# A two-block transformer on one core: retention's projections ahead of MLA attention, MLA on buffers of its own, retention in chunks with states

## The chip, the cores and the metric

The kernel runs on one core of one Trainium2 chip. The metric is the device time of one execution in microseconds (us); the median of three runs stands for a kernel. Engines are named as in the profile: PE (TensorE, matrix products), DVE (VectorE), ACT (ScalarE), POOL (GpSimd) and SP (SyncE, whose queue issues nearly all DMAs).

## The reference, cut to what matters

512 tokens of 1024 features pass a first block (two layers of windowed and full attention, untouched here) and a second block of two layers. Each of these projects the normed input and feeds three mixers (RWKV, retention, MLA attention), whose outputs, side by side, pass one output projection:

```python
for l in range(DEPTH):
    hn = rms_norm_2(h, attn_norm[l])
    proj = hn @ w_in[l]
    ...
    y_a, v_first = rwkv7_mixer(p_a, ...)
    y_b = retention_mixer(p_b, positions)
    y_c = mla_mixer(p_c, positions, ...)
    mix = jnp.concatenate([y_a.astype(h.dtype), y_b.astype(h.dtype), y_c.astype(h.dtype)], axis=-1)
    h = h + mix @ w_out[l]
    hn = rms_norm_2(h, ffn_norm[l])
    gu = hn @ w_gate_up[l]
    h = h + (jax.nn.silu(gu[..., :D_FF_2]) * gu[..., D_FF_2:]) @ w_down[l]
```

Retention (4 heads of 64) is defined in chunks of 128 tokens with a state handed from chunk to chunk; with one decay per head this equals one masked product over all 512 tokens:

```python
inner = jnp.einsum('bhnqd,bhnkd->bhnqk', qc, kc) * dmask[:, None]
inner = jnp.einsum('bhnqk,bhnkd->bhnqd', inner, vc)
kv_chunk = jnp.einsum('bhnkd,bhnke->nbhde', kc * k_dec[:, None, :, None], vc)
def step(R, kv_i):
    return R * chunk_dec[None, :, None, None] + kv_i, R
_, R_prev = lax.scan(step, R0, kv_chunk)
cross = jnp.einsum('bhnqd,nbhde->bhnqe', qc * q_dec[:, None, :, None], R_prev)
y = (inner + cross).transpose(0, 2, 3, 1, 4).reshape(B, S, RET_HEADS, RET_HEAD_DIM)
y = y * lax.rsqrt(jnp.mean(y * y, axis=-1, keepdims=True) + NORM_EPS)
return jax.nn.silu(g) * y.reshape(B, S, RET_DIM)
```

MLA attention has 8 heads (64 + 32 features for scores, 64 for values), causal over the 512 tokens.

## The kernel before

Activations lie with features on the partitions, in eight tiles of 128 x 512. A large product is made of split factors: `load_w` loads a weight (`raw`, two buffers), ACT casts it to `whi`, DVE subtracts to `wlo` (three buffers each); PE multiplies high with high, low with high and high with low. So a 1024 x 128 piece of a projection is 24 matmuls of 512 columns. `H` (tiles `hh`, `hl`) is the normed input of a layer in split form, `mix` (`mh`, `ml`) the mixers' output.

The program text gives the work and the buffers; when the program is built, a scheduler puts the instructions of each engine into one fixed order, in which the engine then runs them. Pools of SBUF tiles and of PSUM banks (`psum`, `bank(tag)`, 8 banks in all) decide when a buffer may be written again.

In `block2`, one layer's mixers run like this:

- `rwkv`, with four PSUM banks `r`, and on its side `mla_inputs`, whose products alternate over the banks `l` and `b` (two each; `self.lb`). MLA's q, k and v go to DRAM (`mlaq`, `mlak`, `mlakr`, `mlav`), RWKV's output to `mix` in DRAM.
- `ret_inputs`, retention's own projections of `H`: four for q and k with a rotary step (`rope`: a shuffle, two products on DVE, one on POOL), one token-wise for v (96 matmuls of 256 columns) and two for the gate g. It is a generator: some of it is called ahead of MLA, the rest after it in the text, and the scheduler uses it as filling within MLA.
- `mla`, head by head: q, k and v come back from DRAM into the tiles of x (`slots`; x itself waits in DRAM as `xd`), ACT casts and DVE subtracts (`qk`). Scores go to the banks `l`, `l`, `m` in turn, DVE takes the row maximum, ACT the exponent, PE turns the result (bank `t`), ACT and DVE split it (`mpt`), PE multiplies with v (bank `o`). After each pair of heads the row sums go to DRAM and back as a broadcast (`rm`, `bc`), POOL multiplies, and SP stores the pair to `mix`.
- `retention`, two pairs of heads: for each pair a table of decays (`dec`, 512 KB) is loaded; per block of 128 keys, scores against all later queries (banks `l`, `l`, `m`), a multiplication by the table on DVE (`rp`), a product with v into `o`.
- `residual`: x comes back, `mix` is loaded and split, and eight pieces of the output projection are added to x, in the banks `b`: 18 matmuls each for the six tiles of RWKV and MLA, and behind them six each for retention's two tiles (`w2outb`), 192 in all.

Of the kernel before, what the change touches and what calls it, by code (L numbers as in the profile page):

```python
# [10 lines left out]
F32 = mybir.dt.float32  # L11
# [9 lines left out]
T = 512  # L21
# [33 lines left out]
class Kern:  # L55
    def __init__(self, tc, d, out, ctx, V):
        self.tc, self.nc, self.d, self.out = tc, tc.nc, d, out
        self.ctx, self.V = ctx, V
        nc = self.nc
        self.uid = 0  # L60
        E = ctx.enter_context
        self.const = E(tc.tile_pool(name="const", bufs=1))
        self.wp = E(tc.tile_pool(name="wp", bufs=2))
        self.tmp = E(tc.tile_pool(name="tmp", bufs=2))
        self.dram = E(tc.tile_pool(name="dram", bufs=1, space=DRAM))
        c = self.const
# [764 lines left out]
    def residual(self, wd, nkt, a, x, gcol, plan, done, norm=None, pre=None):  # L831
# [4 lines left out]
        for ns, segs in plan:  # L836
# [8 lines left out]
            for i, s in enumerate(segs):  # L845
                late = sum(n < KD - W_BUFS for n in ns) if i and len(ns) > 1 else 0
                for j, n in enumerate(ns[late:] + ns[:late]):
                    ps = self.bank()[:, :s.n]
# [732 lines left out]
    def retention(self, l, pool, src, mix):  # L1581
        nc = self.nc
        qk, vs, gs = src
        tags = itertools.cycle("llm")
        for p in range(2):
            q, k, g = qk[p], qk[2 + p], gs[p]
            dec = self.t(pool, [128, 2, T], F32, "dec", 1)
            nc.sync.dma_start(out=dec, in_=self.d["dec"][:, 2 * p:2 * p + 2])
            pso = self.bank("o")
            for j in range(4):  # L1590
                n = T - 128 * j
                ts = []
                for h in range(2):
                    hs = slice(64 * h, 64 * h + 64)
                    ps = self.bank(next(tags))[:, :n]
                    self.mm(ps, k[hs, 128 * j:128 * j + 128], q[hs, 128 * j:], True, True)
                    t = self.t(pool, [128, T], F32, "rp", 3)[:, :n]
                    nc.vector.tensor_tensor(t, ps, dec[:, h, :n], op=ALU.mult)
                    ts.append(t)
                for h in range(2):  # L1600
                    self.mm(pso[64 * h:64 * h + 64, 128 * j:], vs[j][:, 128 * p + 64 * h:128 * p + 64 * h + 64], ts[h], j == 0, j == 3)
# [8 lines left out]
    def mla(self, l, pool, slots, src, mix):  # L1610
        nc = self.nc
        rd = self.dram.tile([4, 2, 4, 128], F32, name=f"rm{l}")
        tags = itertools.cycle("llm")
        ring = {k: itertools.cycle([slots[i] for i in v]) for k, v in dict(f=(2, 3), P=(1, 5, 6, 4), y=(0,)).items()}
        self.fin = iter(())
        steps = [[] for _ in range(sum(MLAG) + 1)]
        for h in range(8):
            if h % 2 == 0:
# [5 lines left out]
                yt = next(ring["y"])  # L1624
                sums = self.t(pool, [128, 8], F32, "sums", 2)
            qk = []
            for nm in "qk":
                f = next(ring["f"])[0:96]
# [11 lines left out]
            for pair in range(2):  # L1640
                for ii in range(2):
                    i = 2 * pair + ii
                    n = 128 * (i + 1)
                    Sp = self.bank(next(tags))
# [5 lines left out]
                    P = next(ring["P"])  # L1650
# [3 lines left out]
                    def turned(P=P, i=i, ii=ii, pair=pair, out=out):  # L1654
                        if ii == 0:
                            out[pair] = [self.t(pool, [128, 4, 256], F32R, "mpt", 4) for _ in range(2)]
# [31 lines left out]
    def block2(self):  # L1688
# [28 lines left out]
        for l in range(2):  # L1717
# [3 lines left out]
            with ExitStack() as es:  # L1721
                es_l = ExitStack()
# [21 lines left out]
                es_r, es_mix, es_ps = (ExitStack() for _ in range(3))  # L1744
                rps = [self.pool(es_r, "ret0", "right")]
                self.lo = "vector"
                inputs = self.ret_inputs(l, rps, H, bc, rs, tab_r)
# [3 lines left out]
                rps.append(self.pool(es_r, "ret", "right"))  # L1751
# [16 lines left out]
            es_r.close()  # L1768
# [13 lines left out]
            self.residual(lambda n, k0, kn: d[f"w2out{l}"][n], 6, mix, X, 1, self.plan([LAT]), None)  # L1782
# [13 lines left out]
            es_mix.close()  # L1796
            es_b = ExitStack()
# [68 lines left out]
def constants():  # L1866
# [29 lines left out]
    df = np.arange(T)[None, :] - np.arange(128)[:, None]  # L1896
    dec = np.where(df[:, None, :] >= 0, np.exp(lg[None, :, None] * np.maximum(df, 0)[:, None, :]), 0.0) / 8.0
# [125 lines left out]
```

## Time and profile before

| what | us |
|---|---|
| median of three runs (3426.10 to 3429.61) | 3428.77 |
| the profiled execution | 3428.67 |
| its span in the trace | 3426.9 |
| PE busy in the span | 3322.7 (97%) |
| DVE, ACT, POOL busy | 1940.2, 1225.8, 498.3 |

The mixers of the second block's first layer run from about 1949 to 2301 us, those of its second from about 2686 to 3038 us:

| stage | first layer, us | second layer, us |
|---|---|---|
| RWKV, MLA's inputs | 184.0 | 184.3 |
| first 24 matmuls of `ret_inputs` | 7.2 | 7.5 |
| MLA attention | 67.3 | 67.3 |
| rest of `ret_inputs` | 24.4 | 24.3 |
| retention, output projection | 69.5 | 69.0 |

Read it so: PE is nearly always busy, so a stage's length is PE's work plus its waits; the other engines count where PE waits for them. In rows of a timeline, the columns are the start, the duration of the group, the engine, the line of the program, the operation, output<-input, tile shape and count, and in brackets the idle time ahead with what ended it.

### The profile page before, as it was taken

The numbers are of one execution on the slowest core, as the hardware profiler recorded it, in microseconds if no ns is written. First come the engines' busy times: TensorE is split into PE (matmuls) and PEld (weight loads), VectorE is DVE, ScalarE is ACT, GpSimd is POOL, SyncE is SP. The second block draws the span as 40 slices with busy tenths as digits, with TensorE's granted clock in tenths as the row PEclk, the third lists the DMA queues.
The fourth block names the chain that finished last, engine by engine and source line by source line (L and its number), as shares of the span: only waits on it lengthen the run. The fifth ranks groups of instructions, "written<-read, shape, count | busy, mean of one in ns | idle before, by whom it ended". The sixth has DMA issues, their size and how long they took to land. (4 is left out here: it accounts for less than half of the span.)

```text
span 3426.9 us, 48765 instructions
## 1 busy us (share of the span) xinstructions
PE 3322.7 (97%) x19304; PEld 2740.8 (80%) x19304; DVE 1940.2 (57%) x3306; ACT 1225.8 (36%) x2178; POOL 498.3 (15%) x430
## 2 busy tenths in 40 slices
PE   7999999999999999999999998999999988999998
PEld 4888888888888888888888876768888766678887
DVE  7667775756444567666333466764434666654333
ACT  3566622312222356634222322632223324433222
POOL 4231100100000201101000332211001332121001
PEclk9999999999999999999999999999999999999999
DMA  6433372434344243353333422422333214333332
GB/s 213 131 121 117 118 264 95 122 111 138 115 136 130 82 125 95 117 176 99 96 90 97 124 66 74 140 94 92 92 96 105 88 53 128 113 88 99 91 98 83
DMA packets 138397, 386.63 MB, mean 113 GB/s; under 512 B 17524, under 2 KB 29300, under 8 KB 138168
## 3 DMA queue, kind: packets, MB, share of 16 engines
q1 hardware_dynamic: 134840, 372.94, 35.5%
q0 software_dynamic: 3328, 10.57, 0.9%
q8 instruction: 152, 2.49, 0.3%
q14 instruction: 77, 0.63, 0.1%
HBM read 332.34 MB, written 43.76 MB: 110 GB/s over the span
## 5 line engine op out<-in xcount | busy, mean ns | idle before, releaser
L137 ACT CAST whi<-raw 128x1024 fp32r<-128x1024 f32 (+3 forms) x436 | 435.7, 999 | 1280.9 <-PE b L146 838.9
L146 PE MATMUL b<-hl,whi 128*128 128x512 f32 (+1 forms) x1760 | 687.1, 390 | 6.1 <-DVE hl L1089 5.1
L138 DVE TENSOR_TENSOR wlo<-raw,whi 128x1024 fp32r<-128x1024 f32 (+2 forms) x397 | 480.7, 1211 | 370.1 <-ACT whi L137 343.7
L146 PE MATMUL b<-hh,whi 128*128 128x512 f32 (+1 forms) x1760 | 687.4, 391 | 2.1 <-ACT whi L137 2.1
L146 PE MATMUL b<-hh,wlo 128*128 128x512 f32 (+1 forms) x1760 | 685.2, 389 | 1.1 <-DVE wlo L138 1.1
L146 PEld LDWEIGHTS b<-hl,whi 128*128 128x128 f32 x1760 | 332.1, 189 | 81.2 <-DVE hl L1089 8.1
L146 PEld LDWEIGHTS b<-hh,whi 128*128 128x128 f32 x1760 | 332.3, 189 | 77.7 <-ACT whi L137 3.1
L146 PEld LDWEIGHTS b<-hh,wlo 128*128 128x128 f32 x1760 | 332.2, 189 | 75.9 <-DVE wlo L138 1.9
L146 PE MATMUL b<-ah,whi 128*128 128x512 f32 (+1 forms) x864 | 317.8, 368 | 0.0
L146 PE MATMUL b<-ah,wlo 128*128 128x512 f32 (+1 forms) x864 | 317.7, 368 | 0.0
L146 PE MATMUL b<-al,whi 128*128 128x512 f32 (+1 forms) x864 | 317.6, 368 | 0.0
L146 PEld LDWEIGHTS b<-ah,whi 128*128 128x128 f32 x864 | 162.3, 188 | 30.0
L146 PEld LDWEIGHTS b<-ah,wlo 128*128 128x128 f32 x864 | 162.3, 188 | 29.8
L146 PEld LDWEIGHTS b<-al,whi 128*128 128x128 f32 x864 | 162.2, 188 | 29.9
L396 DVE SCALAR_TENSOR_TENSOR wlo<-raw,silb 128x1024 f32<-128x1024 f32 x128 | 158.0, 1235 | 47.0 <-DMA raw<-in_ada1b 27.4
L930 DVE TENSOR_TENSOR tm<-tm,b 128x512 f32<-128x512 f32 (+1 forms) x112 | 69.9, 624 | 198.7 <-PE b L146 192.6
L146 PE MATMUL l<-hh,whi 128*128 128x512 f32 (+1 forms) x472 | 176.6, 374 | 0.8 <-DVE stB L685 0.3
L146 PE MATMUL l<-hl,whi 128*128 128x512 f32 (+1 forms) x472 | 174.9, 371 | 0.0
L146 PE MATMUL l<-hh,wlo 128*128 128x512 f32 (+1 forms) x472 | 172.8, 366 | 0.0
L496 DVE TENSOR_TENSOR pt<-t,pt 128x384 fp32r<-128x384 f32 (+2 forms) x272 | 131.1, 511 | 36.7 <-ACT pt L495 34.9
L146 PE MATMUL b<-hc,whi 128*128 128x256 f32 x800 | 141.6, 280 | 0.0
L455 DVE TENSOR_REDUCE st<-S 128x1 f32<-128x768 f32 (+2 forms) x160 | 121.7, 763 | 34.0 <-PE S L146 33.4
(555 smaller groups left out, 5932.9 us busy)
## 6 DMA issues: line engine op xcount, KB each, us to landing
raw<-in_wgu SPq DMA_DIRECT2D x92, 512.0 KB, 3.6
raw<-in_w2gu SPq DMA_DIRECT2D x88, 512.0 KB, 3.5
raw<-in_ada1b SPq DMA_DIRECT2D x48, 512.0 KB, 3.6
raw<-in_w2in SPq DMA_DIRECT2D x38, 512.0 KB, 3.6
raw<-in_ada0b SPq DMA_DIRECT2D x32, 512.0 KB, 3.7
raw<-in_wg SPq DMA_DIRECT2D x32, 512.0 KB, 3.7
raw<-in_w2d SPq DMA_DIRECT2D x32, 512.0 KB, 3.5
raw<-in_wd SPq DMA_DIRECT2D x24, 512.0 KB, 3.6
```

The source lines that it names most:

```text
L137: self.nc.scalar.copy(hi, raw)
L138: getattr(self.nc, self.lo).tensor_tensor(lo, raw, hi.bitcast(F32), op=ALU.subtract)
L146: self.nc.tensor.matmul(out, l, r, start=start, stop=stop)
L396: nc.vector.scalar_tensor_tensor(junk, raw, 0.5, self.silb[:, v], op0=ALU.mult, op1=ALU.mult, accum_out=m[:, w, k, v:v + 1])
L455: nc.vector.tensor_reduce(nm, S[:, lo:hi], axis=AX.X, op=ALU.max, negate=True)
L496: nc.vector.tensor_tensor(o, src, h.bitcast(F32), op=ALU.subtract)
L930: nc.vector.tensor_tensor(b, th, pu, op=ALU.mult)
```

## The change

1. `ret_inputs` runs in full ahead of `mla`; `H` is then given up and made anew after it.
2. `mla` gets buffers of its own: `mf`, `mP`, `my` and two kinds of `mpt` in a pool of its own, in place of the tiles of x. So x can come back from DRAM earlier, and the output projection (`residual`) can begin while MLA runs.
3. PSUM: from the start of the layer on, `b` two banks, `t` two, `o` one, and RWKV three `r` (before: four); `mla_inputs` alternates over `b` and `t`; MLA's scores use `b` alone; when RWKV's buffers close, three banks `w` take the output projection.
4. `retention` works in chunks: scores only within a chunk, states of 64 x 64 from scaled keys (`rkt`), two steps from state to state (`rst`), and a product of states with scaled queries (`rq`). One table of 128 x 1280 (640 KB) is loaded for both pairs.

```diff
-        self.lb = itertools.cycle("lb")
+        self.lb = itertools.cycle("bt")
...
+        tab = self.t(pool, [128, 10, 128], F32, "dec", 1)
+        nc.sync.dma_start(out=tab, in_=self.d["dec"])
...
-            dec = self.t(pool, [128, 2, T], F32, "dec", 1)
-            nc.sync.dma_start(out=dec, in_=self.d["dec"][:, 2 * p:2 * p + 2])
+            nc.gpsimd.tensor_tensor(qd, v4(q)[:, 1:], tab[:, 6 + p].unsqueeze(1).to_broadcast([128, 3, 128]), op=ALU.mult)
+            ps = self.bank("t")
+            for c in range(3):
+                self.turn(v4(ps)[:, c], v4(k)[:, c])
+            kt = self.t(pool, [128, 3, 128], F32, "rkt", 2)
+            nc.vector.tensor_tensor(kt, v4(ps)[:, 0:3], tab[:, 4 + p].unsqueeze(1).to_broadcast([128, 3, 128]), op=ALU.mult)
+            inner = [self.bank("b") for _ in range(2)]
+            for c in range(4):
+                for h in range(2):
+                    self.mm(v4(inner[h])[:, c], v4(k)[hs[h], c], v4(q)[hs[h], c], True, True)
+            st = self.bank("t")[:, :192].rearrange("p (c e) -> p c e", e=64)
+            for c in range(3):
+                for h in range(2):
+                    self.mm(st[hs[h], c], kt[:, c, hs[h]], val(c, h), True, True)
...
+            nc.scalar.copy(R[:, 0], st[:, 0])
+            for c in (1, 2):
+                nc.vector.scalar_tensor_tensor(R[:, c], R[:, c - 1], tab[:, 8 + p, 0:1], st[:, c], op0=ALU.mult, op1=ALU.add)
             pso = self.bank("o")
...
+                    self.mm(v4(pso)[hs[h], c], val(c, h), v4(w[h])[:, c], c == 0, False)
+            for c in range(3):
                 for h in range(2):
-                    self.mm(pso[64 * h:64 * h + 64, 128 * j:], vs[j][:, 128 * p + 64 * h:128 * p + 64 * h + 64], ts[h], j == 0, j == 3)
+                    self.mm(v4(pso)[hs[h], c + 1], R[hs[h], c], qd[hs[h], c], False, c == 2)
...
-                    Sp = self.bank(next(tags))
+                    Sp = self.bank("b")
...
-                self.psum(es, r=4)
-                self.psum(es_l, "right", l=2, b=2)
-                rp = self.pool(es, "rw")
+            self.psum(es_l, "right", b=2, t=2, o=1)
+            self.psum(es_rw, r=3)
...
-                next(inputs)
-            self.psum(es_ps, t=2, o=1, m=1)
+                ri = self.run(self.ret_inputs(l, [retp, retp], H, bc, rs, tab_r))
+            es_H.close()
             with ExitStack() as es:
                 self.stream = "A"
-                self.mla(l, self.pool(es, "mla"), slots, sm, mixd)
+                self.mla(l, self.pool(es, "mla", "right"), sm, mixd)
                 self.stream = "L"
-            self.lo = "vector"
-            ri = self.run(inputs)
+            es_rw.close()
+            self.psum(es_ps, w=3)
```

Three places in the engines' orders, first layer. The first is ACT at the start of MLA. Before, the first casts of v, q and k (`mv`, `qk`) stand behind a weight that is free long before, and among PE's projections:

```order
L137 CAST whi_19912<-raw_19910 128x1024
L1622 CAST mv_19959<-vf_19957 128x8x64
L1635 CAST qk_3683_19964<-x_5145 96x512
L1635 CAST qk_3685_19970<-x_5146 96x512
L137 CAST whi_20701<-raw_20699 128x1024
```

After, on the same engine (`whi` of 128x768 are weights of the output projection, `tm<-rg` is the gate's tanh):

```order
L137 CAST whi_21344<-raw_21342 128x768
L1496 ACTIVATE tm_20214<-rg_20213 128x512
L137 CAST whi_21370<-raw_21368 128x768
L1496 ACTIVATE tm_20250<-rg_20249 128x512
L1642 CAST mv_20261<-vf_20259 128x8x64
L1655 CAST qk_3730_20268<-mf_20266 96x512
L1655 CAST qk_3733_20275<-mf_20272 96x512
```

The cast of `whi_21370`, whose buffer the last projection of `H` reads, and a tanh of that projection's result now stand ahead of the casts that the first scores need.

The second place is SP's queue at the end of MLA's last pair of heads: `rm` and `bc` carry the row sums, `mix` is the pair's store. Before:

```order
L469 DMA rm_19956<-rc_20689 8x128
L473 DMA bc_20692<-rm_19956 64x512 x2
L131 DMA raw_20971<-in_w2in 128x1024
L477 DMA mix_17969<-x_5143 128x512
L131 DMA raw_21237<-in_w2out 128x768
```

After:

```order
L469 DMA rm_20258<-rc_21043 8x128
L473 DMA bc_21046<-rm_20258 64x512 x2
L477 DMA mix_17969<-my_20825 128x512
L1588 DMA dec_21098<-in_dec 128x1280
L1798 DMA tm_21312<-mix_17969 128x512
```

Retention's only table load stands directly behind the last store; before, its two loads stand 40 rows ahead of this and 14 rows behind it.

The third place is PE at the start of retention. Before, with all projections of `H` done:

```order
L146 MATMUL l_21032<-rqk_19909,rqk_20698 128x512
L146 MATMUL l_21036<-rqk_19909,rqk_20698 128x512
L146 MATMUL m_21042<-rqk_19909,rqk_20698 128x384
L146 MATMUL b_21200<-cf,rst_18024 128x128 x3
L146 MATMUL o_21031<-rp_21034,rv_20852 64x512
L146 MATMUL o_21031<-rp_21038,rv_20852 64x512
```

After, from the last value product of MLA on (`w` is the output projection, `rkt` the keys scaled by the table):

```order
L146 MATMUL o_21018<-mpt_3962_21011,mv_20822 128x128
L146 MATMUL w_21322<-mh_21083,whi_21318 128x512
L146 MATMUL w_21348<-mh_21083,whi_21344 128x512
L146 MATMUL w_21374<-mh_21083,whi_21370 128x512
L146 MATMUL w_21322<-ml_21091,whi_21318 128x512
L146 MATMUL w_21322<-mh_21083,wlo_21319 128x512
L146 MATMUL w_21348<-ml_21091,whi_21344 128x512
L146 MATMUL w_21348<-mh_21083,wlo_21345 128x512
L146 MATMUL w_21374<-ml_21091,whi_21370 128x512
L146 MATMUL w_21374<-mh_21083,wlo_21371 128x512
L146 MATMUL t_21118<-rv_20099,rkt_21106 64x64 x2
```

Between MLA's last product and the first that needs the table stand nine matmuls of the output projection; the first score products and transposes of retention stand ahead of these value products. 147 further matmuls of the output projection follow. Of the 240 matmuls of `ret_inputs` that stood 24 ahead of, 64 within and 152 behind MLA, all are ahead of it now; 36 of the output projection stand within it.

## Rows read from the trace of the kernel before

**Rows 1.** The page's first part: busy time, share of the span, instructions.

```profile
PE 3322.7 (97%) x19304; PEld 2740.8 (80%) x19304; DVE 1940.2 (57%) x3306; ACT 1225.8 (36%) x2178; POOL 498.3 (15%) x430
```

**Rows 2.** Table by stretches, first layer: stretch, length, engines' busy times, PE clock, DMA.

```profile
1949.00:2133.00 184.00, 169.90 (x1701) 131.31 (x1699) 111.78 (x265) 46.53 (x79) 59.77 (x54) 0.94 0.23 66
2133.00:2140.20 7.20, 6.04 (x25) 4.53 (x25) 3.80 (x4) 2.32 (x4) 1.30 (x1) 1.00 0.75 204
2140.20:2207.50 67.30, 60.33 (x374) 47.78 (x373) 56.23 (x106) 48.34 (x129) 16.29 (x12) 0.97 0.48 147
2207.50:2231.90 24.40, 24.40 (x153) 21.59 (x151) 8.60 (x11) 6.84 (x11) 4.82 (x3) 1.00 0.36 115
2231.90:2301.40 69.50, 69.06 (x313) 46.52 (x313) 45.47 (x87) 22.69 (x33) 8.43 (x6) 1.00 0.30 95
2209.50:2219.50 10.00, 10.00 (x87) 10.00 (x86) 3.54 (x5) 2.42 (x5) 4.82 (x3) 1.00 0.35 122
```

**Rows 3.** Timeline of PE: first and last of 21 projection matmuls of 512 columns.

```profile
2135.30 0.40 PE L146 MATMUL b<-hh,whi 128*128 128x512 f32 x1
...
2139.97 0.39 PE L146 MATMUL b<-hh,wlo 128*128 128x512 f32 x1
```

**Rows 4.** Groups of DVE in the MLA stage: count, busy us, mean ns, idle before.

```profile
L1636 DVE TENSOR_TENSOR qk<-x,qk 96x512 fp32r<-96x512 f32 x14 | 13.2, 948 | 0.1
...
L138 DVE TENSOR_TENSOR wlo<-raw,whi 128x1024 fp32r<-128x1024 f32 x5 | 6.0, 1202 | 0.0
...
L437 DVE STREAM_SHUFFLE tm<-b 128x512 f32<-128x512 f32 x3 | 2.2, 736 | 0.0
```

**Rows 5.** One line's instructions (L1636, MLA stage): ns min/median/max, first and last start.

```profile
L1636 DVE TENSOR_TENSOR qk<-x,qk x14: 630/676/1801, 2143.9 to 2191.2; 96x512 fp32r<-96x512 f32 x14
```

**Rows 6.** Timelines of ACT and DVE at the start of MLA.

```profile
2135.75 0.62 ACT L1622 CAST mv<-vf 128x512 fp32r<-128x512 f32 x1 [2.10 <-DMA vf<-mlav]
2136.27 1.14 ACT L1635 CAST qk<-x 96x512 fp32r<-96x512 f32 x2
...
2136.92 1.97 DVE L1636 TENSOR_TENSOR qk<-x,qk 96x512 fp32r<-96x512 f32 x2 [1.41 <-ACT qk L1635]
```

**Rows 7.** Timelines of PE and SP at MLA's end; last, landing of the tables' DMAs.

```profile
2205.92 1.61 PE L146 MATMUL o<-mpt,mv 128*128 128x256 f32 x12 [1.22 <-DVE x L503]
...
2203.28 0.35 SPq L469 DMA_DIRECT2D rm<-rc  x1
...
2211.33 0.33 SPq L477 DMA_DIRECT2D mix<-x  x1
...
2241.62 0.33 SPq L1588 DMA_DIRECT2D dec<-in_dec  x1
...
DMA to landing us min/median/max: 3.6/3.6/3.6
```

**Rows 8.** Timeline of PE in retention: scores, successor, value products of 512 and 128 columns.

```profile
2231.93 1.13 PE L146 MATMUL l<-rqk,rqk 64*128 64x512 f32 x4
2232.89 0.81 PE L146 MATMUL m<-rqk,rqk 64*128 64x384 f32 x2
...
2234.93 1.67 PE L146 MATMUL o<-rp,rv 128*64 128x512 f32 x4 [0.36 <-DVE rp L1598]
...
2243.47 0.44 PE L146 MATMUL o<-rp,rv 128*64 128x128 f32 x4
```

**Rows 9.** Groups of PE by shape, from 2231.9 to 2301.4: retention's normalisation.

```profile
L146 PE MATMUL t<-cf,smlA 128*64 128x128 f32 x32 | 2.2, 279 | 0.0
L146 PE MATMUL t<-cf,ry 128*128 128x2 f32 x16 | 2.1, 254 | 0.1
```

**Rows 10.** Timeline of DVE in RWKV: two products consumed in a group.

```profile
2007.32 1.29 DVE L1317 TENSOR_TENSOR A<-r,m 128x512 f32<-128x512 f32 x2 [0.34 <-PE r L146]
```

**Rows 11.** PE's timeline around a gap, and the table by stretches behind it.

```profile
2122.31 1.98 PE L146 MATMUL r<-cf,smlR 128*64 128x128 f32 x16 [3.53 <-DVE smlR L217]
...
2121.30:2132.00 10.70, 9.69 (x33) 6.64 (x34) 4.71 (x11) 0.00 (x0) 0.00 (x0) 0.52 0.44 125
```

More of the change, by code (lines that the diff above doesn't have):

```diff
@@ L829, in merge, with residual @@
                 self.ada_some(1)
-    def residual(self, wd, nkt, a, x, gcol, plan, done, norm=None, pre=None):
+    def residual(self, wd, nkt, a, x, gcol, plan, done, norm=None, pre=None, tag="b"):
         nc = self.nc
@@ L847, in residual @@
                 for j, n in enumerate(ns[late:] + ns[:late]):
-                    ps = self.bank()[:, :s.n]
+                    ps = self.bank(tag)[:, :s.n]
                     self.proj(ws[n], a, s, ps)
@@ L1589, in retention @@
             pso = self.bank("o")
-            for j in range(4):
-                n = T - 128 * j
-                ts = []
+            for c in range(4):
                 for h in range(2):
[L1594 to L1599, printed above, removed]
+                    self.mm(v4(pso)[hs[h], c], val(c, h), v4(w[h])[:, c], c == 0, False)
@@ L1608, in retention, with mla @@
             self.split(y, mix[0]["lat"][6 + p], mix[1]["lat"][6 + p])
-    def mla(self, l, pool, slots, src, mix):
+    def mla(self, l, pool, src, mix):
         nc = self.nc
         rd = self.dram.tile([4, 2, 4, 128], F32, name=f"rm{l}")
-        tags = itertools.cycle("llm")
-        ring = {k: itertools.cycle([slots[i] for i in v]) for k, v in dict(f=(2, 3), P=(1, 5, 6, 4), y=(0,)).items()}
+        take = lambda tag, n: self.t(pool, [128, T], F32, tag, n)
         self.fin = iter(())
@@ L1623, in mla @@
                 nc.gpsimd.tensor_tensor(Vt[:, :, :, 64:128], vf, Vt[:, :, :, 0:64].bitcast(F32), op=ALU.subtract)
-                yt = next(ring["y"])
+                yt = take("my", 1)
                 sums = self.t(pool, [128, 8], F32, "sums", 2)
@@ L1627, in mla @@
             for nm in "qk":
-                f = next(ring["f"])[0:96]
+                f = take("mf", 2)[0:96]
                 if nm == "q":
@@ L1649, in mla @@
                     self.mm(Sp[:, qs], self.identb, self.mle, False, True)
-                    P = next(ring["P"])
+                    P = take("mP", 3)
                     c = 4 * (h % 2) + i
@@ L1655, in turned @@
                         if ii == 0:
-                            out[pair] = [self.t(pool, [128, 4, 256], F32R, "mpt", 4) for _ in range(2)]
+                            out[pair] = [self.t(pool, [128, 2 * pair + 2, 256], F32R, f"mpt{pair}", 2) for _ in range(2)]
                         self.transposed(P, [(128 * kb, kb) for kb in range(i + 1)], *out[pair],
@@ L1720, in block2 @@
             sm = dict(q=DT("mlaq", [8, 96, T]), k=DT("mlak", [8, 64, T]), kr=DT("mlakr", [32, T]), v=DT("mlav", [4, 128, T]))
-            with ExitStack() as es:
-                es_l = ExitStack()
-                self.psum(es, r=4)
-                self.psum(es_l, "right", l=2, b=2)
-                rp = self.pool(es, "rw")
+            es_l, es_rw, es_r, es_mix, es_ps = (ExitStack() for _ in range(5))
+            self.psum(es_l, "right", b=2, t=2, o=1)
+            self.psum(es_rw, r=3)
+            retp = self.pool(es_r, "ret")
+            if True:
+                rp = self.pool(es_rw, "rw")
                 bc, slots = X["lat"][7], X["lat"][:7]
@@ L1743, in block2 @@
                 self.stream = "L"
-                es_r, es_mix, es_ps = (ExitStack() for _ in range(3))
-                rps = [self.pool(es_r, "ret0", "right")]
                 self.lo = "vector"
-                inputs = self.ret_inputs(l, rps, H, bc, rs, tab_r)
                 with ExitStack() as er:
@@ L1781, in block2 @@
                 self.split(t, mix[0]["lat"][i], mix[1]["lat"][i])
-            self.residual(lambda n, k0, kn: d[f"w2out{l}"][n], 6, mix, X, 1, self.plan([LAT]), None)
+            self.residual(lambda n, k0, kn: d[f"w2out{l}"][n], 6, mix, X, 1, self.plan([LAT]), None, tag="w")
             es_ps.close()
@@ L1796, in block2 @@
             es_mix.close()
+            es_r.close()
             es_b = ExitStack()
@@ L1895, in constants @@
     lg = np.log(1.0 - 2.0 ** (-5.0 - np.arange(4)))
-    df = np.arange(T)[None, :] - np.arange(128)[:, None]
-    dec = np.where(df[:, None, :] >= 0, np.exp(lg[None, :, None] * np.maximum(df, 0)[:, None, :]), 0.0) / 8.0
+    n = np.arange(128)
+    df = n[None, :] - n[:, None]
+    dec = np.zeros((128, 10, 128))
+    dec[:, 0:4] = np.where(df[:, None, :] >= 0, np.exp(lg[None, :, None] * np.maximum(df, 0)[:, None, :]), 0.0) / 8.0
+    for h in range(4):
+        own = slice(64 * (h % 2), 64 * (h % 2) + 64)
+        dec[:, 4 + h // 2, own] = np.exp(lg[h] * (127 - n))[:, None] / 8.0
+        dec[own, 6 + h // 2] = np.exp(lg[h] * (n + 1))[None, :]
+        dec[own, 8 + h // 2, 0] = np.exp(lg[h] * 128)
     inv32 = (10000.0 ** (-np.arange(0, 64, 2, dtype=np.float32) / 64.0)).astype(np.float32)
```

15 lines of the change are left out of this document (12 added, 3 removed).

## The prediction

> **What bounds the kernel now.** I read the page first: TensorE (PE) is busy 97% of the span [rows 1]. So the time is PE's instructions plus the few places where PE waits. The next view is the table of stages of one layer's mixer [rows 2]. In its rows to 2301.40 the reader is to compare PE's busy time with the stretch: 184.0 us of RWKV and of MLA's input projections (PE 169.9), 7.2 us in which the first 24 of retention's 240 projection matmuls run, 67.3 us of MLA attention (60.3), 24.4 us with the last 152 of them (24.4), 69.5 us of retention and output projection (69.1). From 2133.0 to 2301.4, where the change works, that is 168.4 us with 159.8 busy: only 8.6 us are idle. The change can win instructions, and it can open waits.
>
> **The change, part by part, for one layer.** Prices: a 512-column projection matmul starts every (2139.97 − 2135.30)/20 = 0.234 us, from the first to the last of 21 of them [rows 3], a 256-column one every 10.0/87 = 0.115 us in the last row of [rows 2].
>
> *Projections ahead of attention.* All 240 of them (144 of 512 columns, 96 of 256) now stand in one run: 144·0.234 + 96·0.115 = 44.7 us. The old first 24 needed 7.2 us for 5.6 us of work, since a weight came late; I keep 1.5 us for that: **46.2 us**. Nothing is saved here, only moved.
>
> *The seam before the first score.* Before, the casts of V, q and k and their subtractions ran from 2135.75 to 2138.9 beside the 24 matmuls [rows 6]: cover. Now PE has nothing between the last projection and the first score. In ACT's order ahead of these casts stands the cast of the third output weight, and its buffer comes free only with the last projection. From that end: weight cast 0.8 (three quarters of a 1024-column cast), gate's tanh and V's cast 0.6 each, two casts of q and k 1.14 together [rows 6], the last subtraction 0.7 [rows 5], and some 0.6 for hand-overs: 4.4, taken as **4.5 us**. Lower bound 3.0, since the first product needs the casts alone; upper 5.5, if the two subtractions take the 1.97 us of [rows 6].
>
> *Attention.* The fill between its steps was 64 projection matmuls, 64·0.234 = 15.0 us; now it is 36 of the output projection, 8.4 us. PE's own work falls from 60.3 to 53.7 us. VectorE (DVE) loses five weight halves (6.0 us) and three rotary steps (2.2 us for the shuffles [rows 4], about as much for each of two products: 6.5), and gains four splits of the mix, two more subtractions of q and k and small things (about 5): from 56.2 busy to about 49. The old idle time of 7.0 us is what chains of reduce, exponent and transpose leave; with two score banks in place of three and less fill I see no reason that it shrinks, and take 53.7 + 7.3 = **61 us**. Bounds: 55 (idle time almost gone) and 67 (the banks bind and the old time stays).
>
> A rule against the trace. The 14 subtractions of q and k take 948 ns in the mean [rows 4] but 676 in the median and up to 1801 [rows 5]: something holds some of them up, and GpSimd was multiplying for the rotary steps in that stage. The Trainium skill (SBUF — State Buffer, "SBUF: two separate sides") says that a DVE operation with two SBUF inputs and a GpSimd operation take one port pair in turn, each for its whole length. By it the rotary work that leaves the stage would give back up to 14·(0.948 − 0.676) = 3.8 us of DVE. The sum would fall by as much only if DVE ended last there; with PE busy 90% of the stage I leave it out.
>
> *The new table.* Here lies the largest new wait. Retention now loads one table of 640 KB, in a place that MLA's buffers held; on SP's queue it stands behind the last store of attention, which waits for GpSimd's last multiplication. In the trace that store left at 2211.33, 3.8 us after the end of the last value products (2207.5) and 8.05 us after the row sums were sent [rows 7]. Before, the first of the two tables was loaded during the first head and waited for nothing of this; the second left at 2241.62, in the middle of the first pair, and PE shows no gap for it. Now: store +3.8 to +4.7, table issued 0.4 later, landing after 3.6 us (512 KB [rows 7]; 640 KB estimated at 3.6 to 4.5), one multiplication of 0.6 on DVE: PE goes on some 9.9 us after the last value product. PE stands in order: it has nine output matmuls (2.1 us) and then the product that needs the multiplied k. So **7.8 us** of stall; bounds 4 (sums sent a good deal earlier) and 9. Behind it on PE wait 147 output matmuls that could have run.
>
> *Retention itself.* The last old stage spends 69.5 − 192·0.234 = 24.6 us on retention, of which normalisation (2.2 and 2.1 busy, less overlap [rows 9]) and the eight small products of a spread are about 4.7. So scores and values took 19.9 us. In chunks, for a pair of heads: scores of 128 columns, two heads at once, as dear as the four records in the first line of [rows 8], whose successor starts 0.96 later: 1.0; eight value products at 0.22 [rows 8], its last line: 1.8; six states of 64 columns at half of that: 0.7; six products with the states: 0.7 to 1.3; transposes and mode changes about 1.4: 5.9, so 11.8 for two pairs. **Saved 8.1 us** (bounds 5 and 11). 2.5 us of it now run before the last value products. DVE has less to do as well; but a chain of transposes, scaling, states and sums is new, and PE passes it in order: 3.0 us of waits.
>
> Rule and row differ once more. In the third line of [rows 8] the value products of two heads in separate column halves took 1.67 us for 2·512 columns, no overlap, while scores in separate row halves took 0.96 for as many. The Trainium skill (TensorEngine Tiling (Array Packing), "Key Properties") says that different tiles run in parallel; by that the value products and states would cost half, 2.5 us a layer less. The sum follows the row.
>
> *After attention*: the nine and 147 output matmuls 36.5, retention 24.6 − 8.1 − 2.5 = 14.0, stall 7.8, waits 3.0, and 2.0 for the clock: after PE idled for 3.53 us its granted clock read 0.52 for about 10 us, the lower level of 1.2 GHz [rows 11], and a stall of 7.8 us invites the same; much of what follows waits anyway. **63.3 us.**
>
> *RWKV.* It has three PSUM banks in place of four. Where four products of a step were consumed in two pairs by DVE, 1.29 us each [rows 10], the fourth must now wait for the first: 0 to 3 us per layer, **1.5**. What else moves in this stretch (earlier loads of x, banks of the MLA inputs) costs nothing: PE's order there is nearly the same and x isn't read before the end.
>
> **Sum.** 46.2 + 4.5 + 61 + 63.3 = 175.0 against 168.4, +6.6; with RWKV +8.1; two layers +16.2. Span 3426.9 + 16.2 = 3443.1; the execution was 1.8 above its span, at 3428.67 practically the median of 3428.77: **3445 us**.
>
> **Rivals.**
> 1. *Faster.* The stall is mostly covered. If the last pair's row sums are sent well before its value products end, the table lands 4 us after them, two of these covered: stall 2, no clock loss, one us of waits (9.8 less than summed); attention falls to 55, as in its bound, and RWKV loses nothing. 168.4 + 8.1 − 9.8 − 6 − 1.5 = 159.2 a layer, so 3410. The decisive point is a stall under about 4 us. For it: PE's order has retention's scores, and other work, ahead of those products. Against it: three transfers stand in a row behind the sums [rows 7].
> 2. *Same.* The parts go half way: attention 57, stall 6, waits and clock 3, RWKV 0.5: 168.4 + 8.1 − 4 − 1.8 − 2 − 1 = 167.7, so 3427.
> 3. *Much slower.* Two score banks bind, attention stays at 67, RWKV loses 3 us and the clock 1.5 more: + 6 + 1.5 + 1.5 on the forecast, 17 us a layer more than now, 3463.
> That the change doesn't do what it says is out: the engines' orders show the run of projections, the chunks and the single load.
>
> **How the numbers follow.** Forecast 0.48, rival 1 0.17, rival 2 0.20, rival 3 0.15. The range is 3418 to 3464: it takes in the bounds of seam, stall and attention, and leaves out most of rival 1 and the tail of rival 3. About 0.2%, 7 us, is what a measurement of this kernel can tell from no change; so faster 0.17, same 0.20, slower 0.63.
>
> **What would show it.** Right: a table of stages with about 46, 4.5, 61 and 63 us; a gap of 7 to 9 us on PE soon after the last value products, released by DVE's multiplication, behind it the table's landing; retention's scores and values near 12 us; a granted clock near half behind the gap. Wrong: a gap under 4 us there, attention at 55 or at 67, or PE waits on bank evictions in RWKV of more than 3 us a layer.

## The result and the profile after

The changed kernel takes 3454.36 us (median of four, 3449.79 to 3462.37) against 3427.44 for the kernel before on the same chip: the ratio is 1.008, 95% interval 1.006 to 1.010. It is slower, by some 27 us where 16 were forecast, and inside the range of 3418 to 3464. The profiled execution took 3453.46 us, its span 3451.7.

The first view is again the table by stretches: start and end, length, busy time and instructions of PE, PEld, DVE, ACT and POOL, PE's granted clock, DMA. The first four rows are the first layer (RWKV with MLA's inputs; retention's projections with the seam; attention; what follows), the last four the second layer:

```profile
1948.70:2130.90 182.20, 170.55 (x1700) 132.25 (x1699) 113.38 (x266) 47.85 (x80) 59.25 (x54) 0.96 0.25 75
2130.90:2179.10 48.20, 45.14 (x242) 38.18 (x240) 25.04 (x32) 13.86 (x19) 12.31 (x9) 1.00 0.44 136
2179.10:2247.30 68.20, 59.09 (x364) 48.35 (x365) 46.11 (x96) 46.86 (x129) 7.94 (x7) 0.88 0.33 101
2247.30:2313.00 65.70, 53.75 (x312) 40.99 (x311) 40.28 (x75) 19.37 (x29) 11.25 (x9) 0.92 0.26 81
...
2695.60:2882.10 186.50, 174.06 (x1699) 131.88 (x1698) 116.03 (x267) 50.47 (x83) 63.40 (x54) 0.96 0.25 72
2882.10:2930.30 48.20, 45.15 (x242) 38.19 (x240) 24.73 (x32) 13.43 (x18) 12.30 (x9) 0.99 0.46 136
2930.30:2998.20 67.90, 59.24 (x363) 48.39 (x363) 45.97 (x95) 46.59 (x129) 7.99 (x7) 0.88 0.34 102
2998.20:3061.30 63.10, 56.08 (x303) 42.51 (x304) 35.41 (x67) 19.45 (x30) 11.29 (x9) 0.86 0.26 84
```

The forecast was 46.2 + 4.5, 61 and 63.3 us. Projections and seam are 2.5 us shorter, the rest behind attention is about as forecast, and attention is 7 us longer: it has lost 28 filling matmuls against [rows 2] and not a microsecond. Its clock is 0.88 where it was 0.97.

The second view is PE's waits from the start of RWKV to the end of the output projection, first layer (waited for, us in total, times, longest):

```profile
PE t L146 <- DVE rkt L1598: 7.5, 1, 7.5
PE t L150 <- ACT mP L459: 5.9, 5, 2.5
PE t L146 <- DVE smlA L217: 3.9, 1, 3.9
PE r L146 <- DVE smlR L217: 3.8, 2, 2.0
PE b L146 <- ACT qk L1655: 3.1, 1, 3.1
```

The table's wait (`rkt`) is the largest, as forecast, and the seam (`qk`) shows with 3.1 us; `smlR` and `smlA` belong to the normalisations of RWKV and of retention. The wait of PE's turning for exponents (`mP`) within attention was part of the idle time of 7.3 us that the prediction carried over, but it has grown. Before, where the exponents lay in tiles of x, the same wait read:

```profile
PE t L150 <- ACT x L459: 1.0, 2, 0.8
```

The timelines of PE, DVE, POOL and SP show the table's wait to the end, as the counterpart of [rows 7]:

```profile
2245.80 1.51 PE L146 MATMUL o<-mpt,mv 128*128 128x256 f32 x12
...
2257.01 0.91 PE L146 MATMUL t<-rv,rkt 128*64 128x64 f32 x12 [7.54 <-DVE rkt L1598]
...
2256.30 0.56 DVE L1598 TENSOR_TENSOR rkt<-t,dec 128x384 f32<-128x384 f32 x1 [7.65 <-DMA dec<-in_dec]
...
2250.46 1.26 POOL L476 TENSOR_TENSOR my<-my,bc 128x512 f32<-128x512 f32 x1 [8.81 <-DMA bc<-rm]
...
2251.75 0.33 SPq L477 DMA_DIRECT2D mix<-my  x1
2252.13 0.42 SPq L1588 DMA_DIRECT2D dec<-in_dec  x1
```

The last value products end at 2247.3; the store follows 4.4 us later (forecast 3.8 to 4.7), the table 0.4 after it, and PE goes on 9.7 us after the products (9.9).

The clock is told by the same table of stretches for four short pieces: the first 10 us of attention, a piece of its middle, the stall for the table, and the wait for `smlA`:

```profile
2179.00:2189.00 10.00, 7.71 (x25) 5.82 (x26) 6.46 (x12) 5.22 (x14) 1.64 (x2) 0.50 0.55 170
2212.90:2219.70 6.80, 5.68 (x24) 5.07 (x25) 4.26 (x9) 4.81 (x13) 0.00 (x0) 0.50 0.31 96
2254.00:2261.00 7.00, 3.99 (x34) 3.19 (x36) 2.83 (x6) 0.83 (x2) 1.96 (x2) 0.52 0.33 116
2274.00:2278.00 4.00, 4.00 (x30) 2.84 (x24) 4.00 (x6) 0.25 (x1) 1.28 (x1) 0.57 0.00 0
```

Each goes with an idle time of PE: the first, second and fourth follow 3.1 us at the seam, 2.5 us of waiting for exponents and 3.9 us for `smlA`; the third begins within the 7.5 us of waiting for the table. In all of them the granted clock is at or near 0.50, the lower level of 1.2 GHz.

### The profile page after: what moved, and what is told of

Same layout as the page of the kernel before. It is cut to its first block, busy times and chain, and to the rows that moved or that the text cites. A ratio compares the mean times of both kernels' runs of the same rounds, so it can differ in the third digit from the quotient of the medians.

```text
span 3451.7 us, 48973 instructions
## 1 busy us (share of the span) xinstructions
PE 3331.9 (97%) x19412; PEld 2763.7 (80%) x19412; DVE 1936.2 (56%) x3294; ACT 1228.3 (36%) x2182; POOL 499.9 (14%) x434
## 5 line engine op out<-in xcount | busy, mean ns | idle before, releaser
L146 PE MATMUL S<-kst,qst 128*128 128x256 f32 (+2 forms) x576 | 137.8, 342 | 2.4 <-issue 1.1
L929 POOL TENSOR_TENSOR tm<-tm,bcf 128x512 f32<-128x512 f32 x44 | 56.7, 1288 | 565.2 <-DVE tm L927 565.2
L146 PE MATMUL l<-hh,whi 128*128 128x512 f32 (+1 forms) x368 | 134.2, 365 | 0.8 <-DVE stB L685 0.3
```

Source lines behind the costliest of these rows:

```text
L146: self.nc.tensor.matmul(out, l, r, start=start, stop=stop)
L929: nc.gpsimd.tensor_tensor(th, th, bc[:, s.off:s.off + n], op=ALU.mult)
```

## The experiments

All are timed beside the kernel before, on the same chip; the ratio is to that, and runs are best compared by it. "Attention" and "behind it" are the first layer's stages as above, in us, from one profiled execution each; that of e5 is its fastest (3407.1 us), that of e4 its slowest (3423.4). "Filling" counts the projection matmuls that the engines' order has within attention, and their time in us at 0.234 for 512 columns and 0.115 for 256 ([rows 2], [rows 3]); in e5, e10 and e15, 36, 28 and 42 of them are token-wise ones of 256 columns.

| run | median us | ratio, 95% interval | filling (us) | attention, clock | behind it |
|---|---|---|---|---|---|
| before | 3427.4 to 3430.8 | 1 | 64 (15.0) | 67.3, 0.97 | 93.9 |
| changed | 3454.4 | 1.0080 [1.0060, 1.0100] | 36 (8.4) | 68.2, 0.88 | 65.7 |
| e1 table early | 3451.2 | 1.0061 [1.0046, 1.0076] | 36 (8.4) | 68.6, 0.88 | 64.6 |
| e7 retention apart | 3432.4 | 1.0004 [0.9992, 1.0015] | 33 (7.7) | 71.0, 0.86 | 51.6 |
| e9 no filling | 3468.9 | 1.0119 [1.0102, 1.0137] | 0 | 68.2, 0.83 | 71.0 |
| e2 three score banks | 3447.9 | 1.0051 [1.0036, 1.0066] | 24 (5.6) | 64.7, 0.90 | 70.5 |
| e11 turning later | 3444.5 | 1.0049 [1.0033, 1.0065] | 36 (8.4) | 63.2, 0.92 | 68.8 |
| e12 one gate as filling | 3422.5 | 0.9984 [0.9971, 0.9996] | 24 (5.6) | 61.5, 1.00 | 64.0 |
| e3 gates as filling | 3419.3 | 0.9966 [0.9955, 0.9977] | 48 (11.2) | 63.7, 0.95 | 70.0 |
| e5 old filling | 3417.0 | 0.9961 [0.9946, 0.9976] | 86 (15.8) | 68.2, 0.95 | 79.9 |
| e10 old filling, three banks | 3422.4 | 0.9978 [0.9968, 0.9988] | 78 (14.9) | 70.6, 0.93 | 81.6 |
| e15 old filling, turning later | 3417.1 | 0.9961 [0.9949, 0.9973] | 92 (16.5) | 71.6, 0.88 | 80.6 |
| e4 before with chunks | 3415.4 | 0.9959 [0.9944, 0.9975] | 63 (14.7) | 63.5, 0.97 | 91.2 |
| e14 the same, turning later | 3414.9 | 0.9958 [0.9946, 0.9970] | 66 (15.4) | 65.6, 0.97 | 92.1 |

### The stall behind attention

The first edit takes the table's load out of the queue behind the last store and gives the table a place of its own:

```diff
             es_H.close()
+            es_rw.close()
+            es_tab = ExitStack()
+            tab = self.t(self.pool(es_tab, "tab"), [128, 10, 128], F32, "dec", 1)
+            nc.sync.dma_start(out=tab, in_=d["dec"])
             with ExitStack() as es:
```

> The changed kernel with one thing altered: the buffers of RWKV are given up ahead of MLA, and the 640 KB table of decays is loaded there, long before attention ends, so that its load no longer stands behind the last store. The theory: the trace after shows PE idle for 7.5 and 6.8 us (first and second layer) until the multiplication by the table; without the wait PE runs on, and the half clock that follows the gap goes too: 14 to 24 us less than the changed kernel's 3454, so 3430 to 3440. The rival, that the chain of transposes, scaling and states would hold PE there anyway: under 6 us less, 3448 or more.

Measured: 3451.2, on the rival's side. PE's waits behind attention (view as above) show why:

```profile
PE o L146 <- DVE rp L1608: 4.5, 1, 4.5
PE t L146 <- DVE smlA L217: 3.9, 1, 3.9
```

and DVE's timeline names the cause, which is neither the table nor the chain of states:

```profile
2254.79 1.29 DVE L1608 TENSOR_TENSOR rp<-b,dec 128x512 f32<-128x512 f32 x2 [4.42 <-DMA mix<-my]
```

The next operation, scores times table, waits for the landing of attention's last store: its result lies where `my` lay, and retention's pool as a whole lies on MLA's. So the table's place in the queue was one of two waits for the same store, one behind the other. The second edit moves the other buffers too:

```diff
-                self.retention(l, self.pool(es, "rets", "right"), ri, mix, tab)
+                self.retention(l, self.pool(es, "rets"), ri, mix, tab)
```

> The changed kernel with the table loaded early, as in the run before with that edit, and besides retention's other buffers in RWKV's place instead of on MLA's. There the multiplication of the scores waited 4.4 us for the landing of MLA's last store, whose tile lay under its result. The theory that the whole stall comes from retention lying on MLA's buffers: PE shows no idle time over 2 us for rkt or rp in either layer, the stage behind attention falls from 65.8 and 63.2 us to 55 to 59, and the time to 3434 to 3441. The rival, that the chain of states holds PE whatever its buffers: 3446 or more.

Measured: 3432.4, better than the theory's band; 1.008 became 1.0004. The stage behind attention in the two layers, and PE's only wait from 2247 to 2310:

```profile
2256.40:2308.00 51.60, 50.60 (x306) 39.00 (x307) 37.10 (x70) 19.36 (x29) 9.34 (x7) 1.00 0.27 88
...
2992.50:3042.60 50.10, 49.29 (x299) 38.30 (x299) 32.42 (x62) 19.29 (x29) 9.89 (x7) 1.00 0.28 91
...
PE w L146 <- DVE ml L143: 1.0, 1, 1.0
```

From 65.7 and 63.1 to 51.6 and 50.1: stall, the wait for `smlA` and the half clock are gone together. 36.5 + 14.0 = 50.5 us was the prediction's sum for this stage without stall, waits and clock. So retention on MLA's buffers, with its table, cost 13 to 14 us a layer there, and by the ratios 26 us of the kernel's time: about all that the change had lost. The second edit without the first was not run.

### The length of attention

Is the stage PE's work plus idle time, as the prediction had it? This edit takes the filling away, by letting each piece of the output projection begin with MLA's last pair:

```diff
+                    if tag == "w":
+                        ws[n] += [(w[0][:, 5:6], w[1][:, 5:6], (5,)), (w[0][:, 0:5], w[1][:, 0:5], range(5))]
+                        continue
```

> The changed kernel with the output projection made to begin each piece with the features of MLA's last pair of heads, which exist only when attention is over; so none of its 36 matmuls stands within MLA. The theory that attention has a length of its own, set by its chain of maximum, exponent, turning and splitting, in which filling is free: the stage stays at 62 to 68 us and the 8.4 us of matmuls are paid behind it: 3460 to 3472. The rival, the prediction's own step, that the stage is PE's work plus idle time: it falls by 8.4 us to about 59.6 and the time stays within 5 us of 3454.

```profile
2182.60:2250.80 68.20, 54.59 (x327) 44.54 (x327) 47.25 (x95) 47.15 (x129) 7.97 (x7) 0.83 0.33 101
...
PE t L150 <- ACT mP L459: 11.0, 12, 1.7
```

The stage is as long with 0 filling matmuls as with 36; 3468.9, the theory's side. There were 36 matmuls fewer, 8.4 us at full clock; PE's waits for exponents went from 5.9 to 11.0 us and the clock from 0.88 to 0.83, so that PE's busy time fell only from 59.1 to 54.6 us. Filling was free there, and what replaced it was waiting and half clock; the 8.4 us a layer were paid behind it (6.7, by the ratios 1.0119 and 1.0080).

Two score banks or three (`tags` gives the banks b, b, m):

```diff
-                    Sp = self.bank("b")
+                    Sp = self.bank(next(tags))
...
+            es_rw.close()
+            self.psum(es_ps, w=2, m=1)
```

> The changed kernel with three PSUM banks for MLA's scores in place of two; the output projection has two in place of three, and by the order only 24 of its matmuls instead of 36 stand within MLA. The theory that the attention stage (68.0 us) is long because PE's clock is at half for 17 of them, after gaps that thin filling and the seam leave: the stage stays at 66 to 70 us and the time within 6 us of 3454. The rival, that two score banks bind: the stage falls to about 61 us, the time by 12 to 16, to about 3440.

Measured: 3447.9, between the two; the stage 3.5 us shorter (3.1 in the second layer), with 12 fewer filling matmuls. These 2.8 us were paid behind it: attention and what follows took 135.2 us together in the first layer against 133.9, and 128.4 against 131.0 in the second. So little of the kernel's gain is seen in these stages. The same edit on top of the old filling:

> The run with the old filling (3417 us) with a third PSUM bank for MLA's scores, taken from the three of the filling. There PE waited 4.5 us a layer for the exponents that free a score bank, with 3 banks in the kernel before with chunks 1.0. The theory: the stage falls from 68 to 64 to 66 us (78 instead of 86 filling matmuls), 3408 to 3415. The rival, that the chain and not the banks makes the wait: within 3 us of 3417.

Measured: 3422.4, not better than 3417.0, and the stage 70.6 instead of 68.2 us. (The 4.5 us that the expectation gives to score banks were the turning's waits for exponents, `PE t L150 <- ACT mP`, not a bank's.) So a third bank gives a little where filling is thin, and two banks are not shown to be what makes the stage long.

The chain itself, with one number and a fourth buffer:

```diff
-MLAG = (1, 1)
+MLAG = (2, 1)
...
-                    P = take("mP", 3)
+                    P = take("mP", 4)
```

> The changed kernel with one number altered: the turning of a step's exponents is written two steps of attention later instead of one (MLAG 2, 1; a fourth buffer mP for it). The theory that attention has a length of its own because its steps follow each other as a chain (PE's waits for exponents are 5.9 and 5.4 us in the two layers): with more room between exponent and turning those waits go, the stage falls from 68 to 62 to 64 us, 3440 to 3447. The rival, that the half clock behind the seam makes the stage long whatever its order: 66 to 69 us, 3450 to 3458.

```profile
2182.00:2245.20 63.20, 57.96 (x363) 46.06 (x363) 47.29 (x95) 46.17 (x129) 8.07 (x7) 0.92 0.37 111
...
PE b L146 <- ACT qk L1655: 3.1, 1, 3.1
PE b L146 <- ACT mP L459: 1.4, 1, 1.4
```

Measured: 3444.5; the stage is 5 us shorter with the same instructions, and the turning no longer waits for exponents. The seam's 3.1 us and the half clock behind it stay; with the wait of 2.5 us the half clock behind that wait is gone too, and the stage's clock goes from 0.88 to 0.92. So the chain from exponent to turning carried these 5 us, partly as waiting and partly through the clock.

### The seam, and the projections ahead

Here `H` is kept, MLA's buffers lie where RWKV's were, and the last steps of `ret_inputs` (8 or 9 of 10 ahead, in the old order 1) are filling, on the banks `w`; the table then loads early, and retention no longer lies on MLA's buffers:

```diff
-                ri = self.run(self.ret_inputs(l, [retp, retp], H, bc, rs, tab_r))
-            es_H.close()
+                self.rtag = "b"
+                inputs = self.ret_inputs(l, [retp, retp], H, bc, rs, tab_r)
+                for _ in range(8):
+                    next(inputs)
+            es_rw.close()
+            self.psum(es_ps, w=3)
             with ExitStack() as es:
...
-                self.mla(l, self.pool(es, "mla", "right"), sm, mixd)
+                self.mla(l, self.pool(es, "mla"), sm, mixd)
...
+            self.rtag = "w"
+            ri = self.run(inputs)
```

> The changed kernel with the projections where they stood before: H is kept, RWKV's buffers and banks are given up ahead of MLA, whose buffers lie there, and all of retention's projections but the first are filling for MLA again (86 matmuls within it by the order, on the three banks w). MLA's scores keep two banks, retention its chunks; the table's load comes early in MLA. The theory (projections ahead of MLA open the seam, thin the filling, lower the clock and bring the table's wait): none of this happens, and the time is that of the kernel before with chunks, 3400 to 3418. The rival, that two score banks and MLA's own buffers make attention long: MLA's stage grows by the 22 more matmuls in it and keeps its 68 us of own length, 3425 to 3440.

Measured: 3417.0, in the theory's band and, by the ratios, 1.2% below the changed kernel: with new buffers and chunks, but without the projections ahead and what came with them, the kernel gains 0.4% on the kernel before. Chunks alone gain as much (e4, below), so no part of it is shown to be the buffers'.

> The run with the old filling (3417 us, 86 projection matmuls within MLA) with only retention's two gate projections left as filling, 48 matmuls, and 192 ahead. H is kept, MLA lies in RWKV's place, the table comes early. The theory of a free filling in a stage of fixed length: the stage stays at 65 to 68 us, 38 matmuls (8.9 us a layer) are paid outside, less what the stage gives back: 3427 to 3436. The rival, that only gaps and stalls made the change slow and the number of filling matmuls doesn't matter: 3412 to 3422.

Measured: 3419.3, the rival's band. The attention stage with 86 matmuls of filling (e5, first layer) and with 48 (both layers):

```profile
2140.50:2208.70 68.20, 61.76 (x397) 50.26 (x396) 56.05 (x107) 49.25 (x131) 20.72 (x15) 0.95 0.44 141
...
2164.50:2228.20 63.70, 59.12 (x379) 47.27 (x377) 48.55 (x97) 45.82 (x127) 7.20 (x5) 0.95 0.33 102
2901.50:2964.50 63.00, 56.70 (x379) 44.56 (x377) 48.40 (x97) 45.85 (x127) 6.59 (x5) 1.00 0.31 94
```

The stage is 4.5 us shorter, in the second layer 5.2. The expectation priced the 38 matmuls that left it at 0.234 us each; but 36 of the 86 are of 256 columns, so the filling fell from 15.8 to 11.2 us, by 4.6. The stage gave back all of that work, and isn't of one fixed length.

> As the run with the gates as filling (3419 us, 48 matmuls within MLA, stage 63.4 us), but with one gate left: 216 projection matmuls ahead, 24 within MLA, so that there is work at the seam but less filling. The theory of a stage with a length of its own, free filling in it and a clock that the seam decides: the stage stays at 62 to 65 us with a granted clock of 0.93 or more, and 24 matmuls more are paid outside, 5.6 us a layer: 3426 to 3432. The rival, that thin filling itself lowers the clock and lengthens the stage: 66 us or more, 3433 or more. The other, that only the seam and stalls matter: 3416 to 3422.

Measured: 3422.5, between the bands of the theory and of "only the seam and stalls matter". The stage and its first 10 us:

```profile
2174.70:2184.70 10.00, 9.27 (x58) 7.25 (x57) 8.04 (x17) 7.38 (x21) 0.00 (x0) 1.00 0.23 63
...
2174.70:2236.20 61.50, 52.36 (x362) 42.43 (x360) 46.77 (x97) 45.51 (x125) 6.42 (x5) 1.00 0.34 102
...
PE t L150 <- ACT mP L459: 6.6, 9, 1.2
```

With work at the seam and only 24 matmuls of filling the clock stays at 1.00 (0.97 in the second layer), and the stage takes 61.5 us although PE waits 6.6 us for exponents. In the changed kernel the first 10 us ran at 0.50 and took 25 instructions instead of 58. So thin filling alone is not what makes the clock fall. PE's idle time within the stage is 9.1 us in both runs (68.2 − 59.1 and 61.5 − 52.4); the 6.7 us between them are busy time. The two pieces at half clock in the changed kernel held 7.7 + 5.7 us of PE's busy time; half of that, an estimate of what the clock cost, is the same 6.7 us. The 12 matmuls more in the changed kernel, 2.8 us, don't show beside it. Strictly, this run differs from the changed kernel in the place of MLA's buffers too; e7, where they lie as in the changed kernel and the stall is mended, keeps seam, half clock (0.86) and length (71.0). The place by itself was not tried.

By the ratios the four runs make a ladder from the changed kernel to the old filling: 26 us for retention off MLA's buffers (e7), 7 for the step to e12, which brings work to the seam but moves MLA's buffers too, 6 for the second gate and 2 for the rest of the filling (e3, e5); in each of the last three steps the two intervals overlap. With 216 of 240 projection matmuls ahead of MLA the kernel is 0.2%, 8 us, behind the old filling. So projections ahead cost little by themselves; most of the time went to retention's place on MLA's buffers. Even with that mended (e7) the kernel is 15 us behind chunks alone (e4, below); seam, half clock and the projections ahead still eat what chunks gain.

### Retention in chunks by itself

The kernel before with the new `retention` and its table alone:

```diff
+        tab = self.t(pool, [128, 10, 128], F32, "dec", 1)
+        nc.sync.dma_start(out=tab, in_=self.d["dec"])
...
-            dec = self.t(pool, [128, 2, T], F32, "dec", 1)
-            nc.sync.dma_start(out=dec, in_=self.d["dec"][:, 2 * p:2 * p + 2])
...
```

> The kernel before with one part of the change alone: retention in chunks with states and its single table; projections, buffers and banks as before. The table's load stands within MLA, and 152 projection matmuls stand between attention and retention. The theory: the products of retention fall from about 20 to 12 us a layer with little waiting, 8 us a layer: 3408 to 3415. The rival, that the chain of states eats the gain with PE waits: 3422 to 3430.

Measured: 3415.4, at the upper edge of the theory. This part of the change is worth 0.4%. With turning later, on top of it and of the old filling:

> The kernel before with chunks (3415 us) with turning two steps later (MLAG 2, 1). PE waited there 1.0 us a layer for exponents with three score banks, and is busy for nearly all of the stage; so little is to be had: 3410 to 3417. If the chain were the limit there too, 3408 or less.

> The run with the old filling (3417 us, waits for exponents 4.5 us a layer) with turning two steps later (MLAG 2, 1; a fourth mP). By the theory of the chain the waits go and the stage falls from 68 to 64 to 66 us: 3408 to 3414. The rival, that with 92 matmuls of filling PE's own work (45 + 21 us) is the limit: 3414 to 3420.

Measured: 3414.9 and 3417.1, nothing in either. In the second the stage even grew to 71.6 us. That PE's work is the limit there isn't shown: 42 of the 92 matmuls are of 256 columns, so the expectation's 45 + 21 us are 45 + 16.5, some 62. PE was busy for 65.0 us at a granted clock of 0.88, against 0.95 in e5; why the clock was lower stays open. e4, e14, e5 and e15 are 0.4% faster than the kernel before, 1.2% than the changed one, and cannot be told from each other.

## Why the prediction was right, and where its sum was off

Direction and range held; the forecast of 16 us was 11 short. Part of the fit is luck: a layer's attention was put 7 us too short, while projections with seam were put 2.5 us too long and RWKV 3.0 to 3.6. Point by point:

- **Projections ahead, seam.** 48.2 us for both against 50.7: the work was right, the seam's gap was 3.1 + 0.7 us instead of 4.5. But its price was not the gap alone: behind it 10 us ran at half clock, and that was not in the sum.
- **Attention: the step that failed.** "53.7 + 7.3 = 61 us." Measured were 59.1 us busy and 9.1 idle. The work came out about as reckoned (59.1 busy at 0.88 is, as an estimate, 52 us at full clock); it took longer because the clock loss was counted behind attention and not within, and that is 5.4 of the 7.2 us; the other 1.8 are idle time. By the prediction's own signs ("attention at 55 or at 67") this part was wrong. Its third rival had the length, but by the score banks, and a third bank took 3.5 us off (e2). The 61.5 us of e12 are near 61 partly by accident: 12 filling matmuls fewer stand against an idle time of 9.1 instead of 7.3. And the model under it, work plus a fixed idle time, holds only where filling is thick: from e5 to e3 the stage gives back all the work that leaves it, from e3 to e12 2.2 and 1.1 of 5.6 us in the two layers, in e9 nothing, and e11 shortens it by 5 us with all of its work.
- **DVE's load** was left out of the sum, rightly: its subtractions of q and k fell from 948 ns ([rows 4]) to 741 in the mean, some 3 us of DVE a layer, and the stage was no shorter for it:

```profile
L1656 DVE TENSOR_TENSOR qk<-mf,qk 96x512 fp32r<-96x512 f32 x16 | 11.8, 741 | 3.5 <-ACT qk L1655 3.5
```

  GpSimd's busy time in the stage fell from 16.3 to 7.9 us. Fewer waits of DVE for GpSimd are what the Trainium skill (SBUF — State Buffer, "SBUF: two separate sides") would lead one to expect from its rule on the shared port pair; no run changes GpSimd's work alone.
- **The table.** 7.5 and 6.8 us against 7.8, by the chain that was named. What was missed is that the store held retention twice: once through SP's order, and behind it through the place of the buffers (e1). Moving the table alone was not enough; both edits together (e7) free the stage.
- **Retention itself** came out near its sum, by errors that cancel. A pair was put at 5.9 us, with eight scores at 1.0 and eight value products at 1.8. In e7 the timeline of PE reads (`b<-rqk` are scores, `t<-rv` states, `o<-rp` value products, `o<-rq` products with the states; each product is two records):

```profile
2253.69 1.16 PE L146 MATMUL b<-rqk,rqk 64*128 64x128 f32 x8
2254.78 1.58 PE L146 MATMUL o<-mpt,mv 128*128 128x256 f32 x12
2256.29 0.57 PE L146 MATMUL t<-rv,rkt 128*64 128x64 f32 x12
2256.78 1.16 PE L146 MATMUL b<-rqk,rqk 64*128 64x128 f32 x8
2257.87 0.49 PE L146 MATMUL b<-cf,rst 128*128 128x128 f32 x2
2258.29 1.09 PE L146 MATMUL o<-rp,rv 128*64 128x128 f32 x16
2259.31 0.87 PE L146 MATMUL o<-rq,rst 64*64 64x128 f32 x12
2260.11 0.93 PE L146 MATMUL b<-cf,rst 128*128 128x128 f32 x6
```

  From the start of one line to that of the next, the eight scores took 1.09 + 1.09 = 2.2 us, the six states 0.49, the eight value products 1.02 and the six products with the states 0.80: 4.5 us, where the sum had 1.0 + 0.7 + 1.8 + (0.7 to 1.3). The score term was mis-sized: it took the time of two products of 512 columns in two row halves ([rows 8], 0.96 us) for eight of 128, and these took more than twice as long. The Trainium skill (TensorEngine Tiling (Array Packing), "Key Properties") says that different tiles can run in parallel, and the prediction preferred the row of before, where the value products did not ([rows 8]). Here the value products in the two column halves do overlap in part: 1.02 us stands between the 1.8 by that row and the 0.9 by the rule.
- **Waits and clock behind attention** were put at 3.0 + 2.0 us; the rows show 3.9 + 0.5 us of waits and two pieces at half clock. Without the table's wait and the 50.5 us of work, 7.7 and 5.8 us are left of the stage in the two layers: a little more than the 5.0.
- **RWKV** was put at +1.5 us for the missing bank; up to the first of the projections it is 182.2 and 186.5 us now and was 184.3 and 188.0. No wait for a bank is among PE's waits there; the price was on the wrong side, its size small.

What stays open: whether the gains of e11 and of e12 in the stage add up (no run has both), why three score banks lengthen the stage with the old filling, why the clock fell in e15, and how much of the difference between e12 and the changed kernel is the place of MLA's buffers.

## What to carry to other kernels

A stage that is a chain over several engines may give back all, some or nothing of the tensor engine's work that is moved out of it: here all where filling was thick (e5 to e3), 1.1 to 2.2 of 5.6 us where it was thin (e3 to e12), nothing where the filling went altogether and the clock fell further (e9). Price a filling by such a run, and by the columns of its matmuls, not by their number. When a pool is laid on another's buffers, look for every later user of that place, not only for the first transfer: the waits stand one behind the other, and mending the first shows the second. And a gap of a few microseconds before a dense stage is to be priced with the half clock behind it: here the gap was 3.1 us, and the 7.7 us of busy time at half clock behind it cost, as an estimate, another 3.9.

## What the runs showed of the hardware

After an idle time of 3.1 us PE's granted clock read 0.50 for 10 us, although PE was busy for 7.7 of them; after 2.5 us it read 0.50 for 6.8 us. With PE at work across the same seam it read 1.00. A wait need not bring half clock: in the second layer of e3 PE waited once for 2.3 us, and the whole stage read 1.00. And value products of 128 columns in the two column halves overlapped in part (1.02 us for eight), while those of 512 columns, a pair at a time, had not; scores in two row halves did the reverse: 0.96 us for two of 512 columns, 2.2 us for eight of 128.
